# Rotary matmul on one core: row-half transposes as 32-bit words, set one by one between the matmuls

## The chip, the cores and the metric

The kernel runs on one core of a Trainium2 chip. Its time is the device time of one launch in microseconds (us): 150.45 us, the median of three runs (150.42 to 150.75).

## The reference

`x` has 16 x 512 rows of 768 fp32 values, `weight` is 768 x 768, and `cos` and `sin` have 512 rows of 64. The product is cut into 12 heads of 64 columns, and the two halves of each head are rotated:

```python
y = np.matmul(x, weight).reshape(batch, seq, n_heads, head_dim)
y1, y2 = y[..., :32], y[..., 32:]
out1 = y1 * cos1 - y2 * sin1
out2 = y2 * cos2 + y1 * sin2
out = np.concatenate([out1, out2], axis=-1).reshape(batch, seq, hidden)
```

## The kernel before

The 8192 rows are 64 tiles of 128 rows. Four tiles make a group `g` (0 to 15), whose 4 x 768 output columns lie side by side in six PSUM banks of 512 fp32 columns, `py`. Two further banks, `pt0` and `pt1`, take transposes.

**From a row to an output.** SyncE or GpSimd loads a tile into `xs`. ScalarE casts it to fp16 into `xc` (line 245), ordered so that columns 6m+2t and 6m+2t+1 of `x` lie next to each other: a 32-bit word for each m (0 to 127) and each t (0 to 2). TensorE transposes the tile into `pt`, and ScalarE copies it to `xt` in SBUF. Then come the matmuls with the fp16 weights `w_sb`, six per output piece, one for each pair (t, e) in `CHUNKS`, each contracting 128 values of the 768. VectorE multiplies finished banks by cosine and sine into `tq` or `w_raw` (line 419), GpSimd adds the two products into `ov` (line 445), and ScalarE or SyncE issues the stores.

**Blocks.** Ten pairs of tiles, the second pair of the groups 5 to 13 and of group 15, take another way: VectorE transposes them as 32-bit words into `xp` (line 299), and TensorE has no transposes for them. Their matmuls read a stationary operand whose elements lie two fp16 apart.

**Two halves.** In tiles 4 to 57 each matmul of 128 rows is split into two of 64 rows: half 0 is partitions 0 to 63, half 1 is 64 to 127, and the two run side by side on the upper and lower half of the array. `walk` (line 344) lists the work of one half for a pair of tiles: six matmuls of 512 columns for each of two banks, and twelve of 256 columns for the middle bank, which straddles the two tiles. Half 0 takes the banks in the order 0, 1, 2, half 1 in the order 2, 0, 1. `both` (line 375) writes out the program order: it takes the next matmul of whichever half has issued fewer columns, by the counters `at[0]` and `at[1]`; `at[1]` starts 1024 columns ahead (`LAG`).

**The transposes.** `turn_rows(i)` (line 261) serves 38 tiles: 6 to 21, the first two of each group from 24 to 57, and 58 to 61. It issues twelve transposes in one go, six (one for each (t, e)) of 64 rows by 128 columns for each half, half r into bank `pt`r; then the copy (line 274) on ScalarE, which reads both banks and writes `xt`. `turns`, called in iteration i of the main loop (lines 683, 689 and 700; from tile 9 on it is the last of them that turns a tile), turns tile i+3. So one tile's transposes stand one tile's matmuls behind the last one's.

**Order and waits.** `Flow.do` (line 42) issues one instruction and gives it the semaphore waits that its reads and writes need: an instruction that writes a buffer waits for all that read the buffer before. The first transpose of a tile into `pt`r therefore waits for the copy of the tile before. Each engine's instructions are issued in program order, and ScalarE's casts, copies and stores share one order.

**The tail.** From tile 58 on the matmuls use all 128 rows (`mm_piece`, line 332). One last piece is added by TensorE (`add_pe`, line 451): a fp32 matmul with the 128 x 128 fp32 identity `ident32`, which lies in the home of weight `w20` and is written there at line 698.

Of the kernel before, what the change touches and what calls it, by code (L numbers as in the profile page):

```python
# [10 lines left out]
FP32 = mybir.dt.float32  # L11
FP16 = mybir.dt.float16
# [4 lines left out]
class Flow:  # L17
# [24 lines left out]
    def do(self, e, make, reads=(), writes=(), dma=None, tick=True, after=0):  # L42
        need = {}
        for k in reads:
            for s, v in self.wrote.get(k, {}).items():
                need[s] = max(need.get(s, 0), v)
        for k in writes:
            for d in (self.wrote, self.readby):
                for s, v in d.get(k, {}).items():
                    need[s] = max(need.get(s, 0), v)  # L50
        if e == "pe":
            need.pop("pe", None)
            if after:
                need["pe"] = after
        waits = self.settle(e, need)
        for s, v in waits[:-1]:
            self.eng[e].wait_ge(self.sem(s), v)  # L57
        i = make(self.eng[e])
        if waits:
            s, v = waits[-1]  # L60
            i.wait_op(self.sem(s), v, "sem-ge")
        name, step = (dma, 16) if dma else (e, 1)
        self.sem(name)
        self.order[name] = len(self.order) + sum(self.count.values())
        at = self.count[name] + step
        if tick or dma:
            i.then_inc(self.sems[name], step)
            self.count[name] = at
            self.known[name, at] = dict(self.seen[e])
        for k in reads:  # L70
            d = self.readby.setdefault(k, {})
            d[name] = max(d.get(name, 0), at)
        for k in writes:
            self.wrote[k] = {name: at}
            self.readby[k] = {}
        return i
# [32 lines left out]
def kernel(  # L109
# [11 lines left out]
    f = Flow(nc, tc)  # L121
    do = f.do
    P = nc.NUM_PARTITIONS

    B, S, H = x.shape
# [5 lines left out]
    NT = H // (2 * P)  # L131
    SB = S // P
    QB = 4
    NG = B * SB // QB
    NTILE = QB * NG
    CHUNKS = [(t, e) for t in range(NT) for e in range(2)]
# [8 lines left out]
    def sbuf(name, shape, dt):  # L145
        return nc.alloc_sbuf_tensor(name, shape, dt).ap()

    NX, NB, NBH, NC, NCP, NXT, NXP, NOV = 10, 3, 3, 5, 2, 8, 4, 4

    ident = sbuf("ident", [P, P], FP16)  # L150
    cold = sbuf("cold", [P, 512], FP16)
    sin_sb = sbuf("sin_sb", [P, SB, D], FP32)
    csn = sbuf("csn", [P, 2, SB, D], FP32)
# [5 lines left out]
    xc_b = [sbuf(f"xc{i}", [P, H], FP16) for i in range(NC)]  # L159
    xd_b = [sbuf(f"xd{i}", [P, 2 * H], FP16) for i in range(NCP)]  # L160
    xt_b = [sbuf(f"xt{i}", [P, NT, 2, P], FP16) for i in range(NXT)]
    xp_b = [sbuf(f"xp{i}", [P, 2 * H], FP16) for i in range(NXP)]
    tq_mem = sbuf("tq", [P, 6144], FP32)
    w_flat = w_raw.rearrange("p t e n -> p (t e n)")
# [7 lines left out]
        v = mem[:, base : base + 2 * n].rearrange("p (j n) -> p j n", j=2)  # L172
        return v[:, :, lo:hi], sorted(keys)

    ident32 = w_flat[:, 3072 : 3072 + P]
    HOMES0, HOMES, HOMESL = (0, 1024, 3072, 4096), (6144, 0, 3072), (0, 1024, 2048, 3072, 4096, 5120)
    ov_b = [sbuf(f"ov{i}", [P, QB * H], FP32) for i in range(NOV)]
    py = nc.alloc_psum_tensor("py", [P, 6 * 512], FP32).ap()
# [1 line left out]
    pt_b = [pt2[:, i] for i in range(2)]  # L180
    HP = P // 2
# [6 lines left out]
    def copy(e, o, i_):  # L188
        return lambda eng: (
            eng.copy(out=o, in_=i_) if e == "act" else eng.tensor_copy(out=o, in_=i_)  # L190
        )
# [57 lines left out]
    def turn(i, e):  # L249
# [8 lines left out]
        do(e, copy(e, xt_b[z], pt), reads=[f"pt{k}"], writes=[f"xt{z}"])  # L258
        xT[i] = (lambda t, h: xt_b[z][:, t, h, :], f"xt{z}")

    def turn_rows(i, e):

        c = xc[i]
        z = ring("xt", NXT)
        src = xc_b[c].rearrange("p (t m e) -> p t e m", t=NT, e=2)
        pts = [pt_b[r].bitcast(FP16)[:, 0 : H // 2].rearrange(
            "p (t e m) -> p t e m", t=NT, e=2) for r in range(2)]
        for t, h in CHUNKS:
            for r in range(2):
                rows = ts(r, HP)  # L270
                do("pe", lambda eng: eng.transpose(  # L271
                    pts[r][:, t, h, :], src[rows, t, h, :], ident[rows, rows]),
                    reads=[f"xc{c}", "ident"], writes=[f"pt{r}"], tick=(t, h) == CHUNKS[-1])
        do(e, copy(e, xt_b[z].rearrange("p t e (r m) -> p r (t e) m", r=2),
                   pt2.bitcast(FP16)[:, :, 0 : H // 2].rearrange("p r (c m) -> p r c m", m=HP)),
           reads=["pt0", "pt1"], writes=[f"xt{z}"])
        xT[i] = (lambda t, h: xt_b[z][:, t, h, :], f"xt{z}")

    def cast_pair(gh, e="act"):
        k = xs[gh]  # L280
# [40 lines left out]
    def pieces(g, s):  # L321

        out_, lo = [], s * H
        for c0, c1, ps, banks, _ in units(g):
            step = 512 if len(banks) > 1 else c1 - c0
            for k, b in enumerate(banks):
                a, z = max(lo, c0 + k * step), min(lo + H, c0 + (k + 1) * step)
                if a < z:
                    out_.append((a, z, ps[:, a - c0 : z - c0], b))
        return out_  # L330
# [27 lines left out]
    def one(g, i, a, z, r, c, opens, start, ends, whole):  # L358
        s, rows, (t, h), bank = i % QB, ts(r, HP), c, a // 512
        get, key = xT[i]  # L360
        after = closed[g, bank] if not opens and c == CHUNKS[0] else 0
        do("pe", lambda eng: eng.matmul(  # L362
            py[:, a:z], get(t, h)[rows], w_sb[rows, t, h, a - s * H : z - s * H],
            start=start, stop=not opens and ends and whole, skip_group_check=True),
            reads=[key, f"w{t}{h}"], writes=[f"ps{bank}"], tick=ends, after=after)
        if ends and whole and opens:
            closed[g, bank] = f.count["pe"]
        if ends and whole and not opens:
            ready.setdefault(g, set()).add(bank)
# [5 lines left out]
    def both(upto):  # L375

        while True:
            n = [(at[r], r) for r in (0, 1) if lines[r]]
            if not n or min(n)[0] >= upto:
                return  # L380
            r = min(n)[1]
            cols, what = lines[r].pop(0)
            at[r] += cols
            one(*what)
            g = what[0]
            for u in units(g):
                k = g, u[0]
                if k not in roped and {b for b in range(u[0] // 512, u[1] // 512)} <= ready.get(g, set()):
                    roped.add(k)
                    rope(g, u)  # L390
# [76 lines left out]
    def store(g, c0, c1, e):  # L467
# [16 lines left out]
    do("pool", lambda eng: eng.affine_select(  # L484
        out=ident, in_=ident, compare_op=mybir.AluOpType.not_equal, fill=1.0,
        base=0, pattern=[[-1, P]], channel_multiplier=1), writes=["ident"])

    order = [0, 1, "w0", 2, "w1", "w2", 3, "w3", "w4", "w5"]
    for k in order:
# [98 lines left out]
    assert not quarters  # L588
    pump()

    rows_on = [False]
    state = {"cast": 4, "turn": 4, "bturn": 0, "pool": 0}
    pairs = sorted(BLOCKS)
# [14 lines left out]
    def turns(upto, most=NTILE):  # L608
        while state["turn"] < min(upto, NTILE) and most > 0:
            i = state["turn"]  # L610
            state["turn"] += 1
            if not is_block(i):
                most -= 1
                (turn_rows if rows_on[0] else turn)(i, "act")

    def bturns(upto):
        while state["bturn"] < len(pairs):
# [50 lines left out]
    for i in range(QB, NTILE):  # L668
        g, s = divmod(i, QB)
        us = units(g)  # L670
        done_to = (s + 1) * H
        rows_on[0] = QB <= i <= QB * LAST
        if i == QB * (LAST - 2) + 2:
            cast_pair((LAST, 1))
            xb_used[0] += 1
        if i < ROWS:
            if s % 2 == 0:
                for r in range(2):
                    lines[r].extend(walk(i // 2, r))
            for n in range(1, 4):  # L680
                both((i - QB) * 4608 + n * 1536)
                if n == (1 if i > QB else 2):
                    turns(i + T_AHEAD, 1)
        if i == ROWS:
            both(NTILE * 4608)
        for n, p in enumerate(pieces(g, s)) if i >= ROWS else ():
            a, z, _, bank = p
            if n == 1 and i < QB * LAST:
                turns(i + T_AHEAD, 1)
            for c in CHUNKS:  # L690
                mm_piece(i, p, c, c == CHUNKS[0], c == CHUNKS[-1],
                         tick=c == CHUNKS[-1])
            for u in us:
                if u[1] == z:
                    rope(g, u)
        bturns(i + (B_AHEAD if i < QB * (LAST - 2) else 9))
        if i == 2 * QB:
            do("pool", lambda eng: eng.tensor_copy(out=ident32, in_=ident),
               reads=["ident"], writes=["ident32", "wr20"])
        turns(i + 1 + (T_AHEAD if i > QB else 2), 1)  # L700
        casts(i + 1 + (C_AHEAD if i > QB else 4), 1 + i % 2)
        pool_loads(i + P_AHEAD)
        for q in stores.get(i, ()):
            store(*q)
        if g == LAST:
            if s == 2:
                store(g, 0, H, "sp")
            if s == 3:
                store(g, H, 2 * H, "act")
# [44 lines left out]
```

## Time and profile before

| what | value |
|---|---|
| median of 3 runs | 150.45 us |
| profiled execution, first to last instruction (span) | 148.2 us |
| left around the span (150.45 - 148.2) | 2.25 us |
| TensorE matmuls (PE), busy | 140.8 us, 95% |
| TensorE weight loads (PEld), busy | 112.7 us, 76% |
| VectorE (DVE), busy | 126.0 us, 85% |
| GpSimd (POOL), busy | 121.8 us, 82% |
| ScalarE (ACT), busy | 79.0 us, 53% |
| DMA, read and written | 27.79 MB and 25.17 MB, 357 GB/s |
| granted TensorE clock | 0.998 |

The profile shows one execution. A time in it counts from its first instruction. A matmul's duration in it holds its passage through the array, in which the next ones already run, so what a stream of matmuls costs is the distance of their starts and not their duration. "Granted clock" is the share of the TensorE clock that the chip's throttle let through. "Idle before, releaser" is the time an engine stood still before an instruction, and what ended it.

### The profile page before, as it was taken

To read this page: it belongs to the slowest core of one execution; us is meant where nothing else is said; L and a number is where in the kernel's file an instruction comes from. 1 tells how busy PE (TensorE), PEld (TensorE's weight loads), DVE (VectorE), ACT (ScalarE), POOL (GpSimd) and SP (SyncE) were. 2 spreads that over 40 slices of the span, in tenths; PEclk is the share of its full clock that TensorE was granted. 3 is DMA by queue.
4 is the path that set the end of the run, shared out by engine and by line. 5 is a ranking of instruction groups with operands and counts; after the bars stand their busy time and mean duration, and the time that the engine had idled before them with its cause. 6 is when DMAs were issued, how large, how long until landed. Compare 5 with 4: busy or idle time off the path is not lost.

```text
span 148.2 us, 4422 instructions
## 1 busy us (share of the span) xinstructions
PE 140.8 (95%) x1948; PEld 112.7 (76%) x1948; DVE 126.0 (85%) x99; ACT 79.0 (53%) x94; POOL 121.8 (82%) x73
## 2 busy tenths in 40 slices
PE   6789999999999999999999999999999999999980
PEld 2335578888888888888888888888888888765860
DVE  0335998886988899899989998999989999999991
ACT  3453898777777933557261915375263919931010
POOL 1000396999999998999999999879699999999990
PEclk9999999999999999999999999999999999999999
DMA  3999999999999999999999999999999999998675
GB/s 124 352 395 403 402 406 398 373 379 296 317 366 330 352 353 277 294 408 287 319 355 397 379 323 358 365 408 324 381 365 337 411 409 416 410 408 333 264 297 180
DMA packets 27555, 51.67 MB, mean 349 GB/s; under 512 B 6160, under 2 KB 13072, under 8 KB 27536
## 3 DMA queue, kind: packets, MB, share of 16 engines
q1 hardware_dynamic: 15824, 28.84, 57.0%
q10 hardware_dynamic: 7360, 20.97, 35.9%
q0 software_dynamic: 4352, 1.57, 8.6%
q8 instruction: 15, 0.25, 0.7%
q14 instruction: 4, 0.03, 0.1%
HBM read 27.79 MB, written 25.17 MB: 357 GB/s over the span
## 4 chain that ended last, share of the span: by engine, by line
PE 78%; DVE 12%; DMA 4%; issue 1%; SPq 1%; DVEq 0%
PE py L362 68%; DVE tq L419 8%; PE py L337 5%; PE pt L271 4%; DMA w_raw<-in_weight_dram 4%; DVE w_raw L419 2%; SPq L210 1%; PE pt L256 1%; DVE ov L445 1%; DVE xs L419 1%; SPq L232 1%; DVE w_sb L190 0%; DVEq L57 0%; SPq L749 0%; SPq L119 0%
## 5 line engine op out<-in xcount | busy, mean ns | idle before, releaser
L445 POOL TENSOR_TENSOR ov<-tq 128x512 f32<-128x512 f32 (+3 forms) x35 | 76.8, 2220 | 20.1 <-DVE tq L419 20.1
L362 PE MATMUL py<-w_sb,xt 64*128 64x256 f16 (+1 forms) x864 | 81.5, 323 | 0.0
L419 DVE TENSOR_TENSOR tq<-py,csn 128x1024 f32<-128x1024 f32 (+2 forms) x51 | 74.4, 1496 | 4.6 <-PE py L362 4.5
L362 PEld LDWEIGHTS py<-w_sb,xt 64*128 64x128 f16 x864 | 59.9, 94 | 11.1 <-DVE tq L419 0.4
L190 ACT COPY xt<-pt 128x768 f16<-128x768 f16 x42 | 33.5, 801 | 47.5 <-PE pt L271 46.3
L362 PE MATMUL py<-w_sb,xp 64*128 64x512 f16 (+1 forms) x432 | 42.7, 323 | 0.0
L190 ACT CAST xc<-xs 128x768 f16<-128x768 f32 x44 | 38.8, 911 | 6.9 <-DMA xs<-in_x_dram 6.7
L419 DVE TENSOR_TENSOR w_raw<-py,csn 128x1024 f32<-128x1024 f32 (+1 forms) x22 | 35.3, 1606 | 4.4 <-PE py L362 4.0
L445 POOL TENSOR_TENSOR ov<-w_raw 128x1536 f32<-128x1536 f32 (+2 forms) x15 | 35.4, 2374 | 1.9 <-DVE w_raw L419 1.9
L362 PEld LDWEIGHTS py<-w_sb,xp 64*128 64x128 f16 x432 | 30.7, 94 | 5.0
L337 PE MATMUL py<-w_sb,xt 128*128 128x256 f16 (+1 forms) x102 | 17.0, 317 | 1.4 <-DVE w_sb L190 1.1
L271 PEld LDWEIGHTS pt<-ident,xc 64*128 64x128 f16 x456 | 14.9, 95 | 1.3 <-issue 0.2
L337 PEld LDWEIGHTS py<-w_sb,xt 128*128 128x128 f16 x102 | 9.2, 98 | 7.4 <-DVE w_sb L190 2.7
L271 PE MATMUL pt<-ident,xc 64*128 64x64 f16 x456 | 14.7, 190 | 0.0
L190 ACT CAST xd<-xb 128x1536 f16<-128x1536 f32 x6 | 9.8, 1634 | 0.0
L225 POOL DMA_DIRECT2D xh<-in_x_dram x16 | 9.4, 591 | 0.0
L190 DVE CAST w_sb<-w_raw 128x768 f16<-128x768 f32 x6 | 3.4, 559 | 3.6 <-DMA w_raw<-in_weight_dram 3.6
L299 DVE STREAM_TRANSPOSE xp<-xd 128x768 f32<-128x768 f32 x6 | 5.8, 970 | 0.0
L190 ACT COPY ov<-py 128x256 f32<-128x256 f32 x1 | 0.4, 372 | 10.1 <-POOL ov L445 10.1
L540 PE MATMUL py<-cold 128*128 128x512 f16 x12 | 4.3, 521 | 1.4 <-DVE cold L482 1.4
L190 DVE COPY xt<-pt 128x768 f16<-128x768 f16 x2 | 1.1, 558 | 4.8 <-PE pt L256 4.8
L299 DVE STREAM_TRANSPOSE xp<-xh 128x768 f32<-128x768 f32 x4 | 4.9, 1234 | 0.0
(23 smaller groups left out, 22.6 us busy)
## 6 DMA issues: line engine op xcount, KB each, us to landing
out_dram<-ov ACTq DMA_DIRECT2D x26, 768.0 KB, 9.6
xs<-in_x_dram SPq DMA_DIRECT2D x44, 384.0 KB, 16.4
xb<-in_x_dram SPq DMA_DIRECT2D x24, 192.0 KB, 16.4
out_dram<-ov SPq DMA_DIRECT2D x4, 768.0 KB, 6.2
w_raw<-in_weight_dram SPq DMA_DIRECT2D x6, 384.0 KB, 6.9
xh<-in_x_dram POOLq DMA_DIRECT2D x16, 96.0 KB, 12.1
out_dram<-ov SPq DMA_DIRECT2D x1, 384.0 KB, 2.3
out_dram<-ov ACTq DMA_DIRECT2D x1, 384.0 KB, 2.3
```

What stands on the lines that cost most here:

```text
L190: eng.copy(out=o, in_=i_) if e == "act" else eng.tensor_copy(out=o, in_=i_)
L210: do(e, lambda eng: eng.dma_start(out=xs_b[k], in_=x[b].rearrange("(p r) h -> r p h", r=SB)[r]), writes=[f"xs{k}"], dma=f"xs{k}")
L225: do(e, lambda eng: eng.dma_start(out=dst[ts(q, R)], in_=src[r, q]), writes=[f"{name}q{q}"], dma=name)
L232: do(e, lambda eng: eng.dma_start(out=w_raw[:, t, h], in_=wv[t, h]), writes=[f"wr{t}{h}"], dma=f"ov{t}_0" if h else f"xb{t}")
L256: do("pe", lambda eng: eng.transpose(pt[:, t, h, :], src[:, t, h, :], ident), reads=[f"xc{c}", "ident"], writes=[f"pt{k}"], tick=(t, h) == ...
L271: do("pe", lambda eng: eng.transpose(pts[r][:, t, h, :], src[rows, t, h, :], ident[rows, rows]), reads=[f"xc{c}", "ident"], writes=[f"pt{r ...
L299: do("dve", lambda eng: eng.transpose(out=dst, in_=src), reads=rd, writes=[f"xp{z}"])
L337: do("pe", lambda eng: eng.matmul(ps, get(t, h), w_sb[:, t, h, a - s * H : z - s * H], start=start, stop=stop), reads=[key, f"w{t}{h}"], w ...
L362: do("pe", lambda eng: eng.matmul(py[:, a:z], get(t, h)[rows], w_sb[rows, t, h, a - s * H : z - s * H], start=start, stop=not opens and en ...
L419: do("dve", lambda eng: eng.tensor_tensor(out=tq.rearrange("p j (h d) -> p j h d", d=D), in0=ps.rearrange("p (h d) -> p h d", d=D) .unsque ...
L445: do(adder, lambda eng: eng.tensor_tensor(out=ov_b[o][:, ds(c0, w)].rearrange("p (h t d) -> p h t d", t=2, d=HD), in0=tq[:, 0].rearrange(" ...
L540: do("pe", lambda eng: eng.matmul(py[:, ts(b, 512)], cold[:, 0:P], cold, start=True, stop=warmed[0] < WARM - 6), reads=["cold"], writes=[f ...
```

## The change

`turn_rows` views the fp16 tile as fp32 words, so that a transpose carries the two values (t, 0) and (t, 1) at once: three transposes of 64 rows by 128 words for each half and tile, in place of six. The identity of these transposes is fp32, `ident32`, now a buffer of its own, written by GpSimd ahead of the loads (and no longer at line 698 in the home of `w20`). In `xt` the two values of a word now lie next to each other, so the matmuls read their stationary operand with a step of two fp16, as those of the blocks do.

The transposes are no longer issued in one go. `turn_rows` puts them into two lists, `pend[0]` and `pend[1]`, and `both` takes one out right behind each 512-column matmul of the same half, and counts 64 columns for it. The copy to `xt` is issued behind the last of the six words. `flush` issues what is left in the lists at once: ahead of the next tile's entry, where half 0 has no matmuls left in its list, and ahead of tile 58.

```diff
     def turn_rows(i, e):
         c = xc[i]
         z = ring("xt", NXT)
-        src = xc_b[c].rearrange("p (t m e) -> p t e m", t=NT, e=2)
-        pts = [pt_b[r].bitcast(FP16)[:, 0 : H // 2].rearrange(
-            "p (t e m) -> p t e m", t=NT, e=2) for r in range(2)]
-        for t, h in CHUNKS:
-            for r in range(2):
-                rows = ts(r, HP)
-                do("pe", lambda eng: eng.transpose(
-                    pts[r][:, t, h, :], src[rows, t, h, :], ident[rows, rows]),
-                    reads=[f"xc{c}", "ident"], writes=[f"pt{r}"], tick=(t, h) == CHUNKS[-1])
-        do(e, copy(e, xt_b[z].rearrange("p t e (r m) -> p r (t e) m", r=2),
-                   pt2.bitcast(FP16)[:, :, 0 : H // 2].rearrange("p r (c m) -> p r c m", m=HP)),
-           reads=["pt0", "pt1"], writes=[f"xt{z}"])
-        xT[i] = (lambda t, h: xt_b[z][:, t, h, :], f"xt{z}")
+        src = xc_b[c].bitcast(FP32).rearrange("p (t m) -> p t m", t=NT)
+        left = [2 * NT]
+
+        def word(r, t):
+            rows = ts(r, HP)
+            dst = pt_b[r][:, t * HP : (t + 1) * HP]
+            do("pe", lambda eng: eng.transpose(dst, src[rows, t, :], ident32[rows, rows]),
+               reads=[f"xc{c}", "ident32"], writes=[f"pt{r}"], tick=t == NT - 1)
+            left[0] -= 1
+            if not left[0]:
+                do(e, copy(e, xt_b[z].rearrange("p t e m -> p (t e m)").rearrange(
+                       "p (t r c) -> p r t c", t=NT, r=2),
+                       pt2.bitcast(FP16)[:, :, 0:H // 2].rearrange("p r (t c) -> p r t c", t=NT)),
+                   reads=["pt0", "pt1"], writes=[f"xt{z}"])
+                v = xt_b[z].rearrange("p t e m -> p (t e m)").rearrange(
+                    "p (t m e) -> p t e m", t=NT, e=2)
+                xT[i] = (lambda t, h: v[:, t, h, :], f"xt{z}")
+
+        for r in range(2):
+            pend[r] += [(r, t, word) for t in range(NT)]
...
     (both)
             one(*what)
+            if cols == 512 and pend[r]:
+                q, t, word = pend[r].pop(0)
+                word(q, t)
+                at[r] += HP
...
+    def flush():
+        while pend[0] or pend[1]:
+            for r in range(2):
+                if pend[r]:
+                    q, t, word = pend[r].pop(0)
+                    word(q, t)
...
     (turns)
-                (turn_rows if rows_on[0] else turn)(i, "act")
+                if rows_on[0]:
+                    flush()
+                    turn_rows(i, "act")
+                    if not lines[0]:
+                        flush()
+                else:
+                    turn(i, "act")
...
         if i == ROWS:
             both(NTILE * 4608)
+            flush()
```

More of the change, by code (lines that the diff above doesn't have):

```diff
@@ L150 @@
     ident = sbuf("ident", [P, P], FP16)
+    ident32 = sbuf("ident32", [P, P], FP32)
     cold = sbuf("cold", [P, 512], FP16)
@@ L173, in products @@
         return v[:, :, lo:hi], sorted(keys)
-    ident32 = w_flat[:, 3072 : 3072 + P]
     HOMES0, HOMES, HOMESL = (0, 1024, 3072, 4096), (6144, 0, 3072), (0, 1024, 2048, 3072, 4096, 5120)
@@ L259, in turn @@
         xT[i] = (lambda t, h: xt_b[z][:, t, h, :], f"xt{z}")
+    pend = [[], []]
     def turn_rows(i, e):
@@ L486 @@
         base=0, pattern=[[-1, P]], channel_multiplier=1), writes=["ident"])
+    do("pool", lambda eng: eng.tensor_copy(out=ident32, in_=ident),
+       reads=["ident"], writes=["ident32"])
     order = [0, 1, "w0", 2, "w1", "w2", 3, "w3", "w4", "w5"]
@@ L696 @@
         bturns(i + (B_AHEAD if i < QB * (LAST - 2) else 9))
-        if i == 2 * QB:
-            do("pool", lambda eng: eng.tensor_copy(out=ident32, in_=ident),
-               reads=["ident"], writes=["ident32", "wr20"])
         turns(i + 1 + (T_AHEAD if i > QB else 2), 1)
```

## The prediction, as it went on record

> **What bounds the kernel now.** I read the page first (span, busy shares, the chain that ended last), then the chain in order of time, then the groups with shapes kept apart, then the timeline around one tile's transposes.
>
> ```profile
> span 148.2 us, 4422 instructions
> ...
> PE 78%; DVE 12%; DMA 4%; issue 1%; SPq 1%; DVEq 0%
> ```
>
> The chain of the longest waits is TensorE. In order of time, over two tiles with transposes and two of a block:
>
> ```profile
> 58.64 5.86 PE py L362 x54
> 64.49 0.17 PE pt L271 x10
> 64.66 1.92 PE py L362 x19
> 66.59 0.20 PE pt L271 x11
> 66.79 5.86 PE py L362 x54
> ```
>
> One half's six transposes take 0.17 us, 29 ns each, and a tile's 4608 columns 1.95 us (5.86 for three), which is 216 ns for 512 columns and 109 for 256. From 18.0 to 130 us the starts of each half follow each other at exactly these distances: with 29, 109 and 216 ns for every instruction less than 0.4 us is left over in either half. The list of waits has no TensorE wait between 20 and 124 us. From 130 us the tiles of full height run as densely, up to the last matmul at 142.8, and the last product on VectorE starts 0.1 us after that one ends. VectorE stands still for PE 8.5 us between 20 and 124 us (4.5 for `tq`, 4.0 for `w_raw`), GpSimd 6.9 us for VectorE. So **each us that TensorE gains or loses reaches the end**, a loss in full, a gain while the 8.5 and 6.9 last.
>
> **What the words save.** 38 tiles x 3 transposes fewer per half x 29 ns = 3.3 us, if a word costs what a transpose of the same 64 columns costs today. Rows for other prices:
>
> ```profile
> L362 PE MATMUL py<-w_sb,xt 64*128 64x512 f16 x432 | 74.7, 376 | 0.0
> L190 ACT COPY xt<-pt 128x768 f16<-128x768 f16 x42 | 33.5, 801 | 47.5 <-PE pt L271 46.3 <-PE pt L256 1.2
> L271 PEld LDWEIGHTS pt<-ident,xc 64*128 64x128 f16 x456 | 14.9, 95 | 1.3 <-issue 0.2 <-ACT xc L190 0.2
> L271 PE MATMUL pt<-ident,xc 64*128 64x64 f16 x456 | 14.7, 190 | 0.0
> L455 PE MATMUL py<-tq,w_raw 128*128 128x256 f32 x4 | 1.1, 393 | 0.0
> L455 PEld LDWEIGHTS py<-tq,w_raw 128*128 128x128 f32 x4 | 0.7, 190 | 0.1
> ```
>
> The only fp32 work on TensorE is L455: two matmuls in four instructions, whose starts lie 216 ns apart for 256 columns. So 64 columns of one such instruction take 54 ns, and two instructions 108. The word lies between 29 and 108; I take 29, the row with the same shape and operation, and keep 108 for the range. The Trainium skill ("TensorE: Matmul & The Clock Gate", Terms, xbus) calls the transpose mode four times faster for fp32; by it 108 would become 27 and the sum would stay.
>
> A fp32 weight load is dearer: the first at L455 starts at 142.75, its matmul streams from 142.86, 109 ns later. Behind a 512-column matmul (216 ns) that is hidden. If both halves share one load path, the other half's load comes up to 27 ns late where it runs 256 columns (109 + 27 - 109); for the some 100 words that meet these that is 2.7 us split over the halves, kept for the range.
>
> At no cost: the copy's new runs (the contiguous copies of L258 take 791 and 799 ns, the strided of L274 798); the step of two in the stationary operand (`xp` has it: 94 ns a load, 376 and 269 a matmul, as `xt`); the 0.3 us of GpSimd for `ident32`, which moves to where GpSimd stands idle (the slices after the first 3.7 us are at 0).
>
> **What the words' new places cost.** Today the transposes of two tiles stand 1.92 us of matmuls apart. A word list can be emptied at once or only near the end of the iteration, since a half in its 256-column stretch (12 x 109 ns = 1.3 us) takes nothing out. But there is one pair of banks `pt` for all tiles: a tile's first word waits until the copy of the tile before has read both. How long that takes, from the timeline:
>
> ```profile
> 64.30 0.36 PE L271 MATMUL pt<-ident,xc 64*128 64x64 f16 x11
> 64.48 0.38 PE L362 MATMUL py<-w_sb,xp 64*128 64x512 f16 x1
> 64.50 0.19 PE L271 MATMUL pt<-ident,xc 64*128 64x64 f16 x1
> ```
> ```profile
> 64.74 0.80 ACT L190 COPY xt<-pt 128x768 f16<-128x768 f16 x1 [3.62 <-PE pt L271]
> ```
>
> The last transpose starts at 64.50, the copy at 64.74 (0.24 later), it takes 0.80, and a load released by ScalarE starts 0.05 after the end (19.41 to 19.46). In sum **1.09 us from a tile's last word to the next one's first**. Today's 1.92 covers it; ScalarE stands idle 46 us for transposes. I wrote out the order that `both` and `pend` give, with 64 columns counted for each word, for all 38 tiles. 204 of the 228 words follow a 512-column matmul, 24 are flushed. Between a tile's last word and the next one's first there are, in the half that comes to it first:
>
> - no matmul (both flushed): tile 8. Stall 1.09 - 0.03 = 1.06
> - one of 512 columns (245 ns with the word): tiles 7, 18, 19, 20, 21, 25, 29, 33. Stall 0.84 each, with 0.33 more in 21, 25 and 33, where the other half had the last word: 7.1
> - two: 16, 17, 57, 59, 60. 5 x 0.63 = 3.1
> - three: 10, 12, 14, 15, 53, 58, 61. 7 x 0.41 = 2.9
> - four: 13, 49. 2 x 0.19 = 0.4
> - more than four, no stall: the 14 others, 24 and 28 among them, and 37, 41, 45.
>
> That is 14.5 us in 23 stalls. Behind the waiting weight load stands all of TensorE's order, the other half's matmuls too. The trace shows such a hold at 18.6, where a wait for a copy (17.80 to 18.60) stands ahead of one half's load:
>
> ```profile
> 17.80 0.80 ACT L190 COPY xt<-pt 128x768 f16<-128x768 f16 x1
> ```
> ```profile
> 18.02 0.33 PEld L362 LDWEIGHTS py<-w_sb,xt 64*128 64x128 f16 x3 [0.32 <-issue]
> 18.72 0.14 PEld L362 LDWEIGHTS py<-w_sb,xt 64*128 64x128 f16 x4 [0.37 <-DVE tq L419]
> ```
>
> Both halves' loads resume together at 18.72. After a stall the fp32 load is bare too: 23 x about 0.09 = 2.0 us; and the words of tiles 6, 8, 10 and 61 that are flushed three in a row follow each other at 109 instead of 29 ns: 0.8 us.
>
> **Sum.** 14.5 + 2.8 - 3.3 = 14.0 us more, the span 162.2, the time (2.25 around the span, as for the median) **164.4 us**. Bounds: no bare loads, 161.6; the wait holds only its own half (against the hold at 18.6), by the same list 10.5 more, 161.0; a word at 108 ns, 20.6 more, 171.0 (stalls shrink a little as words lengthen).
>
> **Rivals.** *Faster, the stalls are not there* (0.10). Place: the first word's wait for the copy. From a distance of 1.09 us on at all 37 places the wait costs nothing, and 3.3 less 0.8 to 1.4 for bare loads remains, of which VectorE's 8.5 us can take all: 147.9 us, at most 147.2. For it: 14 places have that distance by my list. Against it: at the others 0.2 to 0.9 us lie between, less than the copy's 0.80 plus the 0.29 around it, and nothing gives a second pair of banks.
>
> *The wait hidden, but a word dear* (0.04): 108 ns a word and no stalls is 5.3 more, 155.8. L455 alone speaks for the price.
>
> *The halves start in order* (0.07). A word waits for its 512-column matmul to stream. If the other half's next matmul, behind it in the order, had to wait for the word's start, the halves would run one after the other around every word: by the same list with starts in order 30.6 more, 181 us. The trace speaks against it: above, a matmul of L362 starts at 64.48, ahead of a transpose at 64.50, though all twelve transposes come before it in the order; the halves run as two chains. The Trainium skill says the opposite ("TensorE: Matmul & The Clock Gate", Part 3, The mechanism: matmuls keep program order in start and end, strict FIFO). By that rule the time would be this rival's; the row decides against it at distances of 0.02 to 0.1 us, and no row shows 0.2, which a word needs.
>
> *It doesn't do what it says*: words mostly flushed instead of covered. By the order 204 of 228 are covered; no chance of its own.
>
> **Chances.** Forecast 0.78, from 161.0 to 171.0. With the 0.04 at 155.8 the range is 155.5 to 171.5; left out are 147 to 148 and 181. Faster by over 0.2% (about what a measurement of this kernel tells from no change) 0.10, within 0.01, slower 0.89.
>
> **What would show it.** A wait of TensorE's loads for ScalarE's `xt` copy, absent today between 20 and 124 us, some 23 times, 14 to 17 us in all, the longest about 1.1, most of it at the tiles 7 to 33, hardly any from 36 to 53, and again from 57 to 61. 228 transposes in fp32, starts 29 ns (or 54) ahead of the next matmul. TensorE's busy share down to some 88%, VectorE's wait for TensorE up from 8.5 to about 20 us, the last matmul near 157. Wrong it would be if the copies ended ahead of the first words (then the order I wrote out is wrong), if TensorE showed no gaps and VectorE ran into its end (then the gain is real), or if the gaps sat behind every word (then starts are in order or the fp32 load is not hidden).

## The result, and the profile after

The changed kernel takes 167.48 us, the median of four runs (167.17 to 167.92), beside 150.44 us (150.18 to 150.75) for the kernel before: a ratio of 1.113, 95% interval 1.1106 to 1.1155, or 17.0 us more. Forecast were 164.4 us (161.0 to 171.0) and 14.0 more. Single executions of one program can stray by some per cent on this chip (the kernel before took 149.57 to 155.20 us in the eleven beside the runs 5 to 8); the ratios below leave such executions out.

First the page of the changed kernel (span; then the shares of the chain that ended last):

```profile
span 165.8 us, 3964 instructions
...
PE 71%; ACT 10%; DVE 9%; DMA 4%; issue 2%; SPq 1%; DVEq 0%
```

The chain is still TensorE's, but ScalarE now has 10% of it, and before it had none. What it does there, the list of waits from 20 us on tells (who waits, for whom: us in total, times, longest):

```profile
PEld pt L273 <- ACT xt L190: 19.3, 22, 1.2
...
DVE tq L432 <- PE py L371: 12.3, 16, 1.8
...
DVE w_raw L432 <- PE py L371: 7.8, 7, 1.6
```

The first line was absent before: 22 times a weight load of a word waits for the copy of `xt`. VectorE's waits for TensorE grew from 8.5 us to 20.1 by the two lines below it, and to 22.9 with two smaller groups (1.6 and 1.2). The groups (busy, mean ns of one, idle before and its releaser):

```profile
L190 ACT COPY xt<-pt 128x768 f16<-128x768 f16 x42 | 33.4, 798 | 63.2 <-PE pt L273 45.9
L273 PE MATMUL pt<-ident,xc 64*128 64x64 f32 x228 | 42.3, 223 | 10.8 <-ACT xt L190 10.7
L273 PEld LDWEIGHTS pt<-ident,xc 64*128 64x128 f32 x228 | 26.7, 137 | 20.3 <-ACT xt L190 19.3
```

The copy is no slower for its new runs (798 ns, 801 before), and the transposes are 228 in place of 456. One such wait in the chain, in order of time:

```profile
85.35 1.29 PE py L371 x12
86.65 0.05 PE pt L273
86.70 0.02 issue
86.72 0.81 ACT xt L190
87.53 0.04 issue
87.58 0.27 PE pt L273
87.85 5.97 PE py L371 x55
```

A tile's last word, the copy, and the next tile's first word follow each other with nothing between. The timeline of TensorE at the same place shows what stands still meanwhile (start, us, instruction; in brackets how long it stood idle before):

```profile
86.47 0.22 PE L273 MATMUL pt<-ident,xc 64*128 64x64 f32 x1
86.49 0.38 PE L371 MATMUL py<-w_sb,xp 64*128 64x512 f16 x1
87.58 0.27 PE L273 MATMUL pt<-ident,xc 64*128 64x64 f32 x1 [0.71 <-ACT xt L190]
87.58 0.48 PE L371 MATMUL py<-w_sb,xp 64*128 64x512 f16 x2
87.81 0.22 PE L273 MATMUL pt<-ident,xc 64*128 64x64 f32 x1
87.86 0.38 PE L371 MATMUL py<-w_sb,xp 64*128 64x512 f16 x1
```

Both halves resume at 87.58, though only one of them has the word that waits; the other's matmul was due at 86.71 (86.49 + 216 ns). And a word that starts at 87.81 (87.809 with its third digit) lets the next matmul of its half start at 87.865: 56 ns, not the 29 that I had taken.

**Where the 17.0 us are.** I laid every start of the trace beside the program order, half by half. From the first 64-row matmul to the last, half 0 takes 114.8 us before and 131.6 after, 16.7 more. With 216, 109 and 56 ns for each instruction the gaps of half 0 sum to 19.9 us, before to 2.9 (with 29 ns): 17.0 more. 16.25 of it lies at the 22 waits, and 0.84 are the instructions right behind 15 of them, which start 54 to 59 ns late; the rest is -0.09. Three words take 168 ns where six transposes took 174, 0.2 us less for 38 tiles. 17.0 - 0.2 is 16.8, within 0.3 of the medians' difference. The spans of the two profiled executions differ by 17.6 us; the other 0.9 lies ahead of the first 64-row matmul (it starts at 18.04 before and 18.91 after), where no word has run yet.

### The profile page after: what moved, and what is told of

Read it like the earlier page. It is cut to its first block, busy times and chain, and to the rows that moved or that the text cites. A ratio compares the mean times of both kernels' runs of the same rounds, so it can differ in the third digit from the quotient of the medians.

```text
span 165.8 us, 3964 instructions
## 1 busy us (share of the span) xinstructions
PE 147.6 (89%) x1720; PEld 113.8 (69%) x1720; DVE 127.6 (77%) x99; ACT 80.0 (48%) x94; POOL 122.1 (74%) x73
## 4 chain that ended last, share of the span: by engine, by line
PE 71%; ACT 10%; DVE 9%; DMA 4%; issue 2%; SPq 1%; DVEq 0%
PE py L371 61%; ACT xt L190 10%; PE pt L273 5%; DVE tq L432 5%; DMA w_raw<-in_weight_dram 4%; PE py L346 4%; DVE w_raw L432 2%; SPq L210 1%; PE pt L256 1%; DVE xs L432 1%; SPq L232 1%; DVE ov L458 0%; DVE w_sb L190 0%; DVEq L57 0%; SPq L775 0%
## 5 line engine op out<-in xcount | busy, mean ns | idle before, releaser
L432 DVE TENSOR_TENSOR tq<-py,csn 128x1024 f32<-128x1024 f32 (+2 forms) x51 | 75.2, 1500 | 14.4 <-PE py L371 12.3
L371 PE MATMUL py<-w_sb,xt 64*128 64x256 f16 (+1 forms) x864 | 86.1, 323 | 0.0
L273 PE MATMUL pt<-ident,xc 64*128 64x64 f32 x228 | 42.3, 223 | 10.8 <-ACT xt L190 10.7
L371 PE MATMUL py<-w_sb,xp 64*128 64x256 f16 (+1 forms) x432 | 45.0, 323 | 0.0
L273 PEld LDWEIGHTS pt<-ident,xc 64*128 64x128 f32 x228 | 26.7, 137 | 20.3 <-ACT xt L190 19.3
L371 PEld LDWEIGHTS py<-w_sb,xp 64*128 64x128 f16 x432 | 32.1, 95 | 3.6
L555 PE MATMUL py<-cold 128*128 128x512 f16 x12 | 5.0, 586 | 1.4 <-DVE cold L495 1.4
```

What stands on the lines that cost most here:

```text
L273: do("pe", lambda eng: eng.transpose(dst, src[rows, t, :], ident32[rows, rows]), reads=[f"xc{c}", "ident32"], writes=[f"pt{r}"], tick=t == ...
L371: do("pe", lambda eng: eng.matmul(py[:, a:z], get(t, h)[rows], w_sb[rows, t, h, a - s * H : z - s * H], start=start, stop=not opens and en ...
L432: do("dve", lambda eng: eng.tensor_tensor(out=tq.rearrange("p j (h d) -> p j h d", d=D), in0=ps.rearrange("p (h d) -> p h d", d=D) .unsque ...
L555: do("pe", lambda eng: eng.matmul(py[:, ts(b, 512)], cold[:, 0:P], cold, start=True, stop=warmed[0] < WARM - 6), reads=["cold"], writes=[f ...
```

## The experiments

The edits are made to the changed kernel. In the expectations A is the forecast's theory, that the first word of a tile waits for the copy of the tile before. B and C are its rivals on TensorE: a fp32 word that is dear by itself, and halves that must start in program order. Later theories are explained where they come up. The "list" is the forecast's count of matmuls between a tile's last word and the next tile's first, made anew for each variant. The kernel before took 150.28, 150.34 and 150.19 us (medians) beside the runs 1 to 4, 5 to 8 and 9 to 10.

### 1. A shorter copy

```diff
                 do(e, copy(e, xt_b[z].rearrange("p t e m -> p (t e m)").rearrange(
-                       "p (t r c) -> p r t c", t=NT, r=2),
-                       pt2.bitcast(FP16)[:, :, 0:H // 2].rearrange("p r (t c) -> p r t c", t=NT)),
+                       "p (t r c) -> p r t c", t=NT, r=2)[:, :, 0:1],
+                       pt2.bitcast(FP16)[:, :, 0:H // 2].rearrange("p r (t c) -> p r t c", t=NT)[:, :, 0:1]),
                    reads=["pt0", "pt1"], writes=[f"xt{z}"])
...
+    for z in range(NXT):
+        do("pool", lambda eng: eng.memset(xt_b[z], 0.0), writes=[f"xt{z}"])
```

The copy takes the words of t = 0 alone; the other two thirds of `xt` stay zero. TensorE's work and order are unchanged.

> The changed kernel, but each tile's copy from the transpose banks takes only the words of t = 0, 256 of the 768 values (the rest of xt stays zero, so this part of the computation is left out). Theory A (a tile's first word waits for the copy of the tile before): the copy falls from 0.80 to some 0.4 us, every distance from last to first word is released that much earlier, the stalls fall from about 14 to 5 us, and the time is 157 to 159 us. Theory B (the fp32 words themselves hold TensorE, by their loads or by the change of type): nothing changes, 167.5. Theory C (a word holds the other half, because halves start in order): 167.5.

Measured: 157.79 us, ratio 1.049 (1.0427 to 1.0554). From its page and its list of waits:

```profile
L190 ACT COPY xt<-pt 128x256 f16<-128x256 f16 x38 | 14.2, 373 | 68.4 <-PE pt L273 50.9 <-PE py L371 17.5
```
```profile
PEld pt L273 <- ACT xt L190: 9.7, 18, 0.9
```

A copy that is 425 ns shorter (798 to 373) takes 9.7 us off the time, 57% of the loss, with the same words at the same places. A rival that puts the loss on TensorE alone leaves it at 167.5 and is refuted as the main cause.

### 2. Three fp16 words at the same places

```diff
-        src = xc_b[c].bitcast(FP32).rearrange("p (t m) -> p t m", t=NT)
+        src = xc_b[c].rearrange("p (t m e) -> p t e m", t=NT, e=2)
...
-            dst = pt_b[r][:, t * HP : (t + 1) * HP]
-            do("pe", lambda eng: eng.transpose(dst, src[rows, t, :], ident32[rows, rows]),
-               reads=[f"xc{c}", "ident32"], writes=[f"pt{r}"], tick=t == NT - 1)
+            dst = pt_b[r].bitcast(FP16)[:, 2 * t * HP : (2 * t + 1) * HP]
+            do("pe", lambda eng: eng.transpose(dst, src[rows, t, 0, :], ident[rows, rows]),
+               reads=[f"xc{c}", "ident"], writes=[f"pt{r}"], tick=t == NT - 1)
```

It transposes the values (t, 0) alone, half of each tile, with the same waits, copy and order.

> The changed kernel with its order, waits and copies, but each word is a fp16 transpose of the value (t, 0) alone (the values (t, 1) are left out). Same count and places, no fp32 on TensorE but the tail. Theory A: the stalls stay (14 us by the list), the word falls from 56 to 29 ns and the bare load behind a stall goes: 13 us above before, 163 to 164 us. Theory B: the loss goes away, 147 to 150. Theory C: as A, near 164 to 167, with gaps behind each word.

Measured: 163.76 us, ratio 1.0874 (1.0794 to 1.0954), again with 22 waits (19.2 us in the list of waits). The timeline of TensorE at the same tile:

```profile
85.26 0.20 PE L273 MATMUL pt<-ident,xc 64*128 64x64 f16 x1 [0.69 <-ACT xt L190]
85.27 0.41 PE L371 MATMUL py<-w_sb,xp 64*128 64x512 f16 x2
85.49 0.21 PE L273 MATMUL pt<-ident,xc 64*128 64x64 f16 x2
85.52 0.40 PE L371 MATMUL py<-w_sb,xp 64*128 64x512 f16 x2
```

From a word to the next matmul of its half it is 28 to 29 ns here (39 to 41 right behind a wait). What the type costs is thus 167.5 - 163.8 = 3.7 us: 114 words a half at 27 ns more are 3.1, and the late instructions behind the waits sum to 0.9 us with fp32 and 0.25 with fp16, 0.7 more. The waits themselves are as long with fp16 (19.2 and 19.3 us).

### 3. Words behind every matmul

```diff
-            if cols == 512 and pend[r]:
+            if pend[r]:
```

A list now empties over six matmuls in a row, in the stretch of 256 columns too, so that a tile's words end sooner.

> The changed kernel, but a word is taken out behind every matmul of its half, of 256 columns too. A tile's six words are then out within some 0.5 to 0.8 us, and the next tile's first word comes over 1.1 us later. Theory A: four stalls and 1.5 us are left, 152 to 153 us. Theory B: as many fp32 words, 167 or, since loads behind 256 columns (109 ns) are less covered, more. Theory C: as many words, 165 to 168.

The profiled execution took 152.74 us, within the forecast, but its list has 3.9 us in 7 waits where four stalls of 1.5 us were expected; half 0 loses 2.2 us at them, 1.05 of it at tile 57. Three others took 156.9 to 158.2 us; they have no profile, and no ratio is given. That distances to the copy decide agrees with the profiled execution. What the others wait for stays open; the wait at tile 57 is taken up in 6 to 9.

### 4. Words all at once, as the transposes were

```diff
                     turn_rows(i, "act")
-                    if not lines[0]:
-                        flush()
+                    flush()
```

> The changed kernel, but the six words are issued at once at the end of the iteration, where the fp16 transposes stood before. No stall is left by the list. Each half's second and third word follow the one before by the fp32 load, about 110 ns: 0.28 us for a tile against 0.17 before, in all 3.7 us more than before. Theory A: 154 to 155 us. If both halves share one load path, the six loads follow each other: 0.65 us for a tile, 168 us. Theory B: 167 or more. Theory C: 154 to 155.

Measured: 150.66 us, ratio 1.0014 (0.9982 to 1.0047). Its chain in order of time:

```profile
57.18 0.18 PE pt L273 x6
57.36 1.93 PE py L371 x18
59.29 0.20 PE pt L273 x6
59.49 5.85 PE py L371 x54
```

The waits are gone, as A has it: between two tiles' words lie 1.93 us of matmuls again. The size I expected was wrong: I had put the words of one half 109 ns apart, the latency of a bare fp32 load, but three a half take 0.18 us, some 60 ns each. So loads that follow each other overlap. The copy's new runs, the step of two in the stationary operand and the fp32 identity are all in this kernel, so that they cost nothing either. With this the change falls into two parts. **The words by themselves neither gain nor lose** (three at 60 ns in place of six at 29), and **their places cost all of the 17 us**.

### 5. Words held back until the copy can be done

```diff
-            if cols == 512 and pend[r]:
+            if cols == 512 and pend[r] and at[r] >= free[0]:
...
+                free[1] = max(at)
...
                     flush()
+                    free[0] = free[1] + GAP
                     turn_rows(i, "act")
```

`GAP` is 2700 columns, some 1.14 us of matmuls, counted from the last word of the tile before.

> The changed kernel with one edit: a tile's first word is not taken out before both halves are 2700 columns (1.14 us) past the last word of the tile before. The words stay behind 512-column matmuls, as many as the list lets, the rest is flushed. Theory A (the wait for the copy): by the list three stalls of 2.0 us in all are left, near the start and the end, and words cost what the fp16 transposes did (56 against 2 x 29 ns), so 2.0 us above before, 152 to 153 us. Theory B (the fp32 words hold TensorE): 167, as many words as in the changed kernel. Theory C (halves in order): 165 or more, since most words still stand behind 512 columns.

Measured: 152.88 us, ratio 1.0173 (1.0118 to 1.0228), with 3.6 us in 5 waits. As expected: the words are still spread, and with the distance restored where the lists allow it, 14.6 of the 17 us go. What is left are stalls of 0.58, 1.24 and 0.40 us in half 0 at the tiles 7, 8 and 10, whose words are flushed near to each other, and one of 0.52 us at 125.5 (tile 57); the list had given three stalls and 2.0 us.

### 6 and 7. Both remedies, and words behind every matmul with one flush at the end

```diff
-            if cols == 512 and pend[r]:
+            if pend[r] and at[r] >= free[0]:
...
-                    if not lines[0]:
+                    if i >= ROWS + 3:
                         flush()
```

This is the edit of 6, on top of 5. Kernel 7 has the same second line, and the condition of 3.

> The same distance of 2700 columns, words behind matmuls of 256 columns too, and no flush where half 0's list is empty. Theory A: 0.8 us of stalls left, 150.8 to 151.5 us; no gain, since three words at 56 ns cost a half 168 ns for a tile against six transposes at 29, 174. A gain of 3 us would need a word at 29 ns. Theory B: 167. Theory C: 165 or more.

> Words behind every matmul of the half, without the distance, and without the flush where half 0's list is empty. By the list four stalls of 1.3 us in all: 1.5 us above before, 151.5 to 152.5 us by theory A; 157 if the three later runs of the first kernel of this kind (156.9 to 158.2, against 152.7 in its profiled run) come from the kernel itself; 167 by theory B.

Measured: 156.43 us (ratio 1.0393, 1.0347 to 1.0438) and 155.7 us (1.0337, 1.0277 to 1.0397). Both are 3 to 6 us over what the list gave. In kernel 6 most of it lies in one place. Stretches of 4 us (busy time and count of PE, PEld, DVE, ACT and POOL; granted clock; DMA share; GB/s):

```profile
122.00:126.00 4.00, 1.09 (x13) 0.54 (x8) 2.55 (x3) 2.96 (x4) 4.00 (x4) 1.00 1.03 414
126.00:130.00 4.00, 3.85 (x35) 3.07 (x37) 2.86 (x3) 2.48 (x4) 1.64 (x3) 0.62 1.04 417
```

And ScalarE's timeline there:

```profile
123.04 0.89 ACT L190 CAST xc<-xs 128x768 f16<-128x768 f32 x1 [2.40 <-DMA xs<-in_x_dram]
...
123.84 1.56 ACT L190 CAST xd<-xb 128x1536 f16<-128x1536 f32 x1
...
125.30 0.79 ACT L190 COPY xt<-pt 128x768 f16<-128x768 f16 x1
```

TensorE is busy for 1.09 of 4 us: the first word of tile 57 starts at 126.15, when the copy of tile 56 ends, 3.2 us after it was due and 3.4 us after the last start. The copy runs at 125.30, but the last word that it needs had started at 121.53. It stands in ScalarE's order behind a cast that waits 2.40 us for its load, and behind the cast of a pair. In the kernel before the copy of tile 56 comes first and these two casts after it. A copy is issued where the last word of its tile is issued, so spreading the words also moves the copy back past ScalarE's other work: **theory D**, a second way in which the new places cost. In kernel 7 the same copy runs at 125.52, and the wait is 3.47 us. After the wait in kernel 6, 512 columns take 427 ns in place of 216 for 3.4 us, at a granted clock of 0.5 (0.62 as the mean of the stretch), which costs about half of that time, 1.7 us. A second wait is of the same kind: the copy of tile 18 stands behind a cast that waits for its load (2.35 us in kernel 6, 1.65 in 7), and half 0 loses 1.45 and 0.73 us. Why the casts wait for their loads there, and in the kernel before do not, stays open.

### 8. Six fp16 transposes, spread

```diff
-        left = [2 * NT]
+        left = [4 * NT]
...
-            pend[r] += [(r, t, word) for t in range(NT)]
+            pend[r] += [(r, th, word) for th in CHUNKS]
```

Here `word` issues the transpose of the kernel before, one of six a half, and the copy is that of the kernel before, behind the twelfth.

> The placement alone: the six fp16 transposes of each half as before the change, each set behind a 512-column matmul of its own half, with the copy behind the twelfth. No fp32. Twelve places are needed where six were, so a tile's transposes spread further, and the distance to the next tile shrinks: by the list 26 stalls of 22.7 us in all, 24.8 above before. Theory A: 174 to 176 us. Theory B (the fp32 words): about 150, nothing is left of the loss. Theory C: slower, but by the transposes (456 instead of 228), with gaps behind each.

Measured: 176.91 us, ratio 1.1778 (1.174 to 1.1817). From its list of waits:

```profile
PEld pt L275 <- ACT xt L190: 27.4, 26, 1.3
```

Without any fp32 word the places alone cost 26.6 us (the list gave 24.8, so that the time is 0.9 us over the range expected). Six items for each list last longer than three, so less is left between two tiles. B, which sees nothing to lose here, is refuted a second time: 4 has the words without the spreading, and 8 the spreading, over twice as many places, without the words.

### 9. The copy ahead of the casts

```diff
-    C_AHEAD, T_AHEAD, B_AHEAD, P_AHEAD = 5, 3, 4, 20
+    C_AHEAD, T_AHEAD, B_AHEAD, P_AHEAD = 4, 3, 4, 20
...
-        if i == QB * (LAST - 2) + 2:
+        if i == QB * (LAST - 2) + 3:
             cast_pair((LAST, 1))
...
-        bturns(i + (B_AHEAD if i < QB * (LAST - 2) else 9))
+        bturns(i + (B_AHEAD if i < QB * (LAST - 2) else 8))
```

On top of kernel 7: casts come one iteration later, so that they stand behind the copy in ScalarE's order.

> The kernel of e7 (a word behind every matmul of its half), with ScalarE's order mended: casts one tile later and the last pair's cast one iteration later, so that the copy of tile 56 stands ahead of the cast of tile 58 and of the last pair's cast, as it did before the change. Theory D (what e6 and e7 lose over the list is the copy of tile 56, which stands behind two casts that wait for loads, and the half clock after that stall): the stall of 3.5 us and the half clock go, 1.1 us of stalls near the start are left, 151.3 to 152.0 us. Rival (words behind 256 columns cost more than the list says, or the later loads stall TensorE anyway): 154 to 157, as e7.

The profiled execution took 151.67 us. The copy of tile 56 now runs at 120.22, ahead of the casts, the first word of tile 57 waits for nothing, and the clock stays whole. D holds there. What is left is 0.8 us of stalls near the start and 1.3 us at the first word of tile 58: the copy of tile 57 now stands behind the pair's cast, which waits 0.61 us for its load. But of ten executions only three lie at 151.55 to 151.88 us, a ratio of 1.0082 (1.0017 to 1.0147), and the other seven at 153.9 to 157.6. None of the long ones was profiled, so what they wait for stays open.

### 10. Both mended

```diff
                 word(q, t)
-                at[r] += HP
...
-                    if i >= ROWS + 3:
+                    if i < 9 or i >= ROWS + 3:
                         flush()
```

On top of 9: words are not counted, so that the program order of the matmuls no longer slips against that of casts and loads from tile to tile, and the first tiles flush at once.

> As e9, and the words not counted in the issue counters (so that casts and loads keep their place against the matmuls), and words flushed at once for the tiles turned before iteration 9. By the list 0.5 us of stalls are left, near the end. Theory A with D: 150.4 to 151.2, no faster than before, since a word costs as much as two fp16 transposes. If the words do save something once nothing waits: 147 to 149.

Measured: 150.49 us, ratio 1.0012 (0.9983 to 1.0041), all twelve executions between 150.2 and 151.4. One wait is left in its list of waits:

```profile
PEld pt L273 <- ACT xt L190: 0.8, 1, 0.8
```

So words can be spread at no loss, and with no gain: behind a matmul a word still takes its 56 ns of TensorE. The spread over executions of 3, 7 and 9 didn't appear in these twelve; whether the slip or the early waits had made it wasn't tried alone. No kernel here beats the one before. A second pair of `pt` banks, which would take the wait away at its root, wasn't tried: it needs two banks beside the eight that the kernel uses.

## Why the prediction was right, and where its sizes were off

**The bound** held: what TensorE lost reached the end, 16.7 us at the halves and 17.0 in the time.

**The stalls, 14.5 us in 23.** Right in 22 of 23 places, within 0.2 us. The loop of last word, copy and next first word, 1.09 us by the trace of before, less the matmuls between, gave these, in the half that has the waiting word:

| tiles | forecast each | measured each |
|---|---|---|
| 8 | 1.06 | 1.13 |
| 7, 18, 19, 20, 29 | 0.84 | 1.02, 0.83, 0.83, 0.89, 0.87 |
| 21, 25, 33 | 0.95 | 1.02, 1.01, 0.87 |
| 16, 17, 57, 59, 60 | 0.63 | 0.62 |
| 10, 12, 14, 15, 53, 58 | 0.41 | 0.40, 0.44, 0.40, 0.40, 0.40, 0.40 |
| 13, 49 | 0.19 | 0.19 |
| 61 | 0.41 | no wait |

These sum to 14.4 us, 14.1 by the forecast for the same 22. But half 0 as a whole loses 16.2 at them: where the other half has the waiting word, half 0's own next matmul is often due earlier than that word, and it stands still for longer. The forecast counted each wait by its word alone.

**The wait holds both halves**: right (both resume at 87.58). The row at 18.72, from which I read it, names VectorE as the releaser; that product had started at 18.27, and what ended the wait was the copy, at 18.60. By the lower bound, a wait for its own half alone, 161.0 was to come.

**A word at 29 ns: wrong, 56.** I took the row of the same shape (fp16, 29) over the row of the same type (L455, 54). The type decided. The saving of 3.3 us became 0.2: this term alone is the 3 us by which the forecast was low.

**Bare loads, 2.8 us: too much.** I had 0.09 us behind each wait and 109 ns for words in a row. It was 0.056 behind 15 waits of half 0, 0.8 us, and 55 to 68 ns in a row: 109 is how long one load takes to be ready, not how often one can follow another. In sum: 16.25 + 0.84 - 0.23, less 0.09 unassigned, in place of 14.5 + 2.8 - 3.3. Two errors, 1.7 too little and 2.0 too much, nearly cancel, which is luck, and the third shows.

**The fp32 load behind a 512-column matmul is hidden**: right; the word follows its matmul after 216 ns.

**The rivals.** "The stalls are not there" fell by the 22 waits. "The wait hidden, but a word dear" fell by experiment 1, and a word takes 56 ns, half of the 108. The factor of four that the Trainium skill gives the transpose mode for fp32 ("TensorE: Matmul & The Clock Gate", Terms, xbus), by which it would be 27, is not seen here. (Its own prices, 114 words at 108 ns against 228 transposes at 29, give 5.7 us and not 5.3; the forecast's sum doesn't use it.) "The halves start in order" fell too: behind the words that don't wait no gap is over 26 ns, and the sum would be 181. A word of half 1 that starts at 93.87 stands, in the program order, ahead of a matmul of half 0 that starts at 93.71. The order of starts that the Trainium skill states ("TensorE: Matmul & The Clock Gate", Part 3, The mechanism) thus doesn't hold between the two halves of this kernel, at the 0.16 us of that pair any more than at the 0.02 to 0.1 that the trace of before showed. What does hold up both halves is a load that waits for a semaphore.

**What the forecast didn't see** is theory D. It costs nothing in the changed kernel, where the copy of tile 56 stands behind the same two casts, but they are done before its last word, and it is waited for 0.62 us, as by the list. It costs 3.2 and 3.5 us in kernels 6 and 7, which had mended the first cause.

## What to carry to other kernels

When a burst of work that fills a buffer is spread out, measure the loop of last writer, reader and next first writer, and count what is left between two bursts: 1.92 us between two tiles covered a loop of 1.09, and 0.2 to 0.9 did not. The reader moves with the last writer, past all that its own in-order engine has to do, so look at its queue as well. And where two rows price an operation, one by its type and one by its shape, keep both: here the type's (54 ns) was right and the shape's (29) wrong. Take a chain of loads from rows of a chain, not from the latency of one.

## What the runs showed of the hardware that was not expected

- A fp32 transpose of 64 columns takes 56 ns, a fp16 one 29: three words of 32 bits cost what six fp16 transposes cost (168 and 174 ns).
- A fp32 weight load that nothing covers delays its matmul by 56 ns more (109 to 115 ns from word to word right behind a wait), but six loads in a row, two halves by turns, follow each other at 55 to 68 ns in each half, three in 0.18 us (experiment 4).
- After a pause of 3.38 us between two starts of TensorE (122.77 to 126.15, kernel 6) the granted clock was 0.5 for 3.4 us, from 126.99 on; after one of 3.62 us at the same place in kernel 7 it was 1.00 in the stretch from 126 to 130 us. The length of the pause alone doesn't decide it.
